# A hybrid decoder layer: two groups of turns issued sooner, three roots' Newton steps on GpSimd, the second gate weight and half of its projections in the first stage

## The chip, the cores and the metric

The kernel runs on one core of one Trainium2 chip. Its time is the device time of one execution in microseconds (us). Before the change the median of 3 runs is 1174.29 us (1173.09 to 1176.38). The engines are PE (TensorE), DVE (VectorE), ACT (ScalarE), POOL (GpSimd) and SP (SyncE, which here only issues DMAs). PEld is PE's loading of weights.

## The reference, cut to what matters

One sequence of 2048 rows with 1024 columns. A modulation is computed from `c`, the rows are normalised, and one wide projection feeds two attentions: eight heads of a forgetting attention (FoX) and eight query heads with two key and value heads of a sliding-window attention with a window of 128. Each branch is gated, and both go through one output projection.

```python
mod = jax.nn.silu(c) @ w_ada[l] + b_ada[l]
shift, scale, gate = jnp.split(mod, 3, axis=-1)
h = rms_norm(x, g_pre[l]) * (1.0 + scale[:, None, :]) + shift[:, None, :]
proj = h @ w_in[l]
qa, ka, va, fa, za, qb, kb, vb, zb = jnp.split(proj, split_points, axis=-1)
oa = forgetting_attention(qa, ka, va, fa + b_fgate[l]) * jax.nn.silu(za)
qb, kb = rope(qb, positions), rope(kb, positions)
ob = sliding_window_sink_attention(qb, kb, vb, sinks[l]) * jax.nn.silu(zb)
y = jnp.concatenate([oa, ob], axis=-1) @ w_out[l]
x = x + gate[:, None, :] * rms_norm(y, g_post[l])
```

What the change touches lies in the first stage: the root of `rms_norm`, the transposing of `h`, and the projections `kb` (keys), `vb` (values) and `zb` (gates of the sliding-window heads).

## The kernel before

**Precision.** Every fp32 operand of a large product is split into two f16 parts, a high and a low one, and a product is three matmuls (high by high, high by low, low by high) into one PSUM bank. A weight gets a power of two from its largest value as its scale, the rows `h` one from a bound on their size.

**Groups and units.** The 2048 rows are four groups of 512 (`ci` 0 to 3). A projection of one key (a weight of 128 columns: `kb`, `vb`, `zb0` to `zb3`, `qb0` and so on) for one group is eight units; a unit of `proj_units` (L325) is one k of 128 columns and three matmuls of 512 columns (L339). Behind the eighth unit stands an evacuation: `evac_rope` (L718) for keys and queries, with a copy on ACT, the cosine product on DVE, and seven ticks later the sine product (L746) with rows that a DMA has swapped; `evac_z` (L370) for gates, with a tanh on ACT (L383) and the product on DVE (L379), whose result POOL's queue stores to DRAM. A unit that holds a PSUM bank keeps it until its evacuation has read it; there are three such banks (`bk`).

**Turns.** `turn(ci, k)` (L418) brings one k of a group into the layout that the projections need: PE transposes four 128x128 tiles of the normalised rows `xt` into a PSUM tile `px` (L422, five of them), ACT scales and shifts them with `Gp` and `Shp` into `hf`, for even k also into the high part (L428), and DVE makes the low part by a subtraction (L433), for odd k after a cast to the high part (L432). Group 0's turns stand in the opening code: five are issued ahead of the code that computes `bmx`, `bm`, `pH`, `Gp` and `Shp` (its two small PE instructions are the transpose of `bmx` into bank 0 and the matmul of L644), and turns 5, 6 and 7 each follow when a `px` comes free. The turns of group ci+1 are strewn as extra units among the projections of group ci, at the places that the list `at_` gives.

**Root and normalisation.** ACT sums the squares of a group's rows (`squares`), `rsqrt_parts` (L97) takes the inverse root by an integer estimate and three Newton steps, on four columns, 13 operations of DVE in all. `root(ci)` runs it at one stroke; the root of group 1 is taken a step at a time between group 0's turns. `normal(ci)` multiplies the rows by the root, on DVE for groups 1 to 3.

**A weight's way.** Eight functions prepare a weight: `w_load` (L216, a DMA of POOL's queue), `w_max` (DVE takes the maximum of each partition, L222, and POOL's queue stores it to DRAM as `mx_d`, L225), `w_back` (POOL's queue loads it as a row on all partitions, `mxr`, L230), `w_scale` (DVE reduces the row, L241, and works out the scale), `w_high` (ACT, L256), two times `w_low` (DVE, L262) and `w_done`.

**What sets the order.** The order on each engine is the order of issue in the code. `add(key, units)` appends units to one long list `punits`. When a key is first added, its eight preparing functions are put into `events` at slots ahead of the first unit: 42, 31, 21, 12, 9, 7, 5 and 4 units ahead, for `qb0` and `zb1` the first four 16, 14, 12 and 4 sooner. `fill(n)` (L1083) runs the next n units, and ahead of each the functions that stand at its slot. In the first stage every second unit is followed by a `tick`, which runs what `after(n, f)` has put off by n ticks: the evacuations and the ACT and DVE halves of the turns. Squares, roots and normalisations of groups 2 and 3, and `spread` (the cosine and sine rows of a group), are events too.

**Stages.** The first stage has the list `kb`, `vb`, `zb0` for groups 0 to 2, `kb`, `vb` for group 3, then `qb0` for group 0, the rest of `zb0`, `qb0` for group 1, and the first group of `zb1`: 144 units, the 24 turns counted (`N_PRO`). In the profile it ends at 157 us. Then 32 windows of the sliding-window attention follow to 431 us. A window (`Pair`) has scores on PE (L871), maxima on DVE, exponentials on ACT (L893), transposes on PE (L900), their copy on ACT and a subtraction on DVE, four `affine_select` of POOL (L909, L911) and the product with the values on PE (L924); between these steps lie 296 units of the remaining `qb`, `zb`, and `va` projections, spread evenly over the 32 windows. The list `others` holds the `zb` and `va` projections in order, four per key: `zb0`, `zb1`, `va0`, `zb2`, `zb3`, `va1`, `va2`. The FoX stage and the output projection come behind.

Of the kernel before, what the change touches and what calls it, by code (L numbers as in the profile page):

```python
# [10 lines left out]
F32 = mybir.dt.float32  # L11
# [8 lines left out]
P = 128  # L20
# [23 lines left out]
def hybrid_layer(  # L44
# [46 lines left out]

    def rsqrt_mean(dst, ss, n):

        for _ in rsqrt_parts(dst, ss, n):
            pass

    def rsqrt_parts(dst, ss, n, more=None):  # L97
        v = sm(n, "rs_v")
        if more is None:
            V.tensor_scalar(v[:], ss, 1.0 / D, EPS, op0=ALU.mult, op1=ALU.add)  # L100
        else:
            V.scalar_tensor_tensor(v[:], ss, 1.0 / D, more, op0=ALU.mult, op1=ALU.add)
        y = sm(n, "rs_y")
        h = small.tile([P, n], I32, tag="rs_h", name="rs_h")
        V.tensor_scalar(h[:], v[:].bitcast(I32), 1, None, op0=ALU.logical_shift_right)
        V.tensor_scalar(y[:].bitcast(I32), h[:], -1, 0x5F3759DF, op0=ALU.mult, op1=ALU.add)
        V.tensor_scalar(v[:], v[:], -0.5, None, op0=ALU.mult)
        for it in range(3):
            yield
            t = sm(n, "rs_t")  # L110
            if n == 1:
                V.scalar_tensor_tensor(t[:], y[:], y[:], v[:], op0=ALU.mult, op1=ALU.mult)
            else:
                V.tensor_tensor(t[:], y[:], y[:], op=ALU.mult)
                V.tensor_tensor(t[:], t[:], v[:], op=ALU.mult)
            y2 = dst if it == 2 else sm(n, "rs_y")
            V.scalar_tensor_tensor(y2[:], t[:], 1.5, y[:], op0=ALU.add, op1=ALU.mult)
            y = y2
# [287 lines left out]
    def root(ci):  # L406
        ss, rst = rstd[ci]
        rsqrt_mean(rst, ss[:], 4)

# [7 lines left out]

    def turn(ci, k):  # L418

        px = ps_x.tile([P, CH], F32, tag="x", name="px")  # L420
        for u in range(4):
            PE.transpose(px[:, u * P:(u + 1) * P], xt[ci * 4 + u][:, k * P:(k + 1) * P], ident[:])  # L422
        hf = hst.tile([P, CH], F32, tag="hf", name="hf")
        hi, lo = hT[ci][:, 0, k, :], hT[ci][:, 1, k, :]

        def scaled():
            for dst in ([hi] if k % 2 == 0 else []) + [hf[:]]:
                A.activation(dst, px[:], AF.Identity, scale=Gp[:, k:k + 1], bias=Shp[:, k:k + 1])  # L428

        def split():  # L430
            if k % 2:
                V.tensor_copy(hi, hf[:])  # L432
            V.tensor_tensor(lo, hf[:], hi, op=ALU.subtract)  # L433

        return scaled, split
# [17 lines left out]
    with tc.manual_schedule():  # L453
# [186 lines left out]

        PE.transpose(bk[0][0:1, 0:P], bmx[:], ident[:])
        bm = st.tile([1, 1], F32, name="bm")
        V.tensor_reduce(bm[:], bk[0][0:1, 0:P], axis=AX.X, op=ALU.max)
# [6 lines left out]

        V.tensor_scalar(pfl[:], ipH[:], 0.5, None, op0=ALU.mult)
        root1 = rsqrt_parts(rstd[1][1], rstd[1][0][:], 4)
        for k in range(KT):
            turned[k][0]()
            turned[k][1]()
            if k >= 2:
                next(root1, None)
            if k + 5 < KT:
                turned.append(turn(0, k + 5))
        V.tensor_reduce(mxs[:, 2:3], wq["zb0"][0][:], axis=AX.XY, op=ALU.max, apply_absolute_value=True)  # L660
# [279 lines left out]
    def add(key, us):  # L940
        if key not in pkeys and key not in ("kb", "vb"):
            at = len(punits) - {"za3": 4}.get(key, 20 if key[:2] == "za" else 0)
            for n, (lead, f) in enumerate(((42, lambda: w_load(key, pieces(key))), (31, lambda: w_max(key)),
# [42 lines left out]
    for ci in range(NCH):  # L986
# [24 lines left out]
    add("qb0", qb_units(0, 1))  # L1011
    add(*others[4])
    N_PRO = len(punits)
    for n in range(4):
        at_slice(N_PRO + 20 + 3 * n, lambda: next(fx["sums"], None))
    qbs = [(f"qb{c_ // 4}", qb_units(c_ // 4, c_ % 4)) for c_ in range(2, 16)]
    n_o = 5
    for n, (key, us) in enumerate(qbs):
        add(key, us)
        lim = 5 + 5 * (n + 1) // 4 if n + 1 < len(qbs) else len(others)  # L1020
        for key2, us2 in others[n_o:lim]:
            add(key2, us2)
        n_o = lim
# [705 lines left out]
```

## Time and profile before

| | us |
|---|---|
| median of 3 runs | 1174.29 (1173.09 to 1176.38) |
| the profiled execution | 1176.95 |
| its span, first to last instruction | 1175.2 |
| PE busy | 1127.3 (96%) |
| DVE busy | 935.1 (80%) |
| ACT busy | 662.0 (56%) |
| POOL busy | 192.6 (16%) |

The page belongs to one profiled execution, 1176.95 us, which lies 2.66 us above the median; every time of the trace is of that execution. Times in a row of the timeline are the start in us from the span's start, then the duration in us, the engine, the line (L) of the kernel, the operation, and output<-input with partitions, elements and type; a bracket at the end gives the idle time ahead of the instruction and what ended it. A row of the groups has busy time and mean ns of one behind the first bar, and the idle time of the engine ahead of such instructions behind the second. The granted PE clock is what the chip's throttle let TensorE have, as a share of full speed.

### The profile page before, as it was taken

The page shows a single profiled execution, that of the slowest core. Times are in us where ns is not written, and L with a number is a line of the kernel's source. Part 1 is how long each engine was busy: PE and PEld are TensorE (multiplying, and loading weights), DVE is VectorE, ACT ScalarE, POOL GpSimd, SP SyncE. Part 2 cuts the span into 40 slices and gives each one's busy share as a digit, 9 for nine tenths or more (in the row PEclk, how much of TensorE's full clock was granted, in tenths as well). Part 3 has the DMA queues.
Part 4 walks back from the last instruction along what each step waited for, and adds up shares of the span by engine and source line. Part 5 has one row for each costly group of instructions (what it writes and reads, how often), then busy time and mean ns, then how long its engine had stood idle before and what let it go on. Part 6 is the DMA issues. An engine that isn't in the chain of part 4 may idle for free.

```text
span 1175.2 us, 26821 instructions
## 1 busy us (share of the span) xinstructions
PE 1127.3 (96%) x10637; PEld 671.1 (57%) x10637; DVE 935.1 (80%) x2167; ACT 662.0 (56%) x1150; POOL 192.6 (16%) x293
## 2 busy tenths in 40 slices
PE   5899999999899999999999999999999999999997
PEld 2465555755457986555555555555556555544444
DVE  7876668688786757788888999888897897778885
ACT  2784445454554531476766767666776788543332
POOL 1000135535445531001000100001000000000000
PEclk9899999999999999999999999999999999999999
DMA  9745433414324323513425422223311237586743
GB/s 332 280 124 87 78 93 73 91 51 106 90 65 89 73 43 75 81 47 95 74 66 60 111 43 74 61 44 73 52 33 47 68 86 231 137 213 199 195 144 108
DMA packets 123481, 120.19 MB, mean 102 GB/s; under 512 B 64948, under 2 KB 100828, under 8 KB 123356
## 3 DMA queue, kind: packets, MB, share of 16 engines
q1 hardware_dynamic: 112088, 85.69, 27.0%
q0 software_dynamic: 10832, 32.50, 13.8%
q8 instruction: 83, 1.36, 0.6%
q14 instruction: 42, 0.34, 0.1%
q10 hardware_dynamic: 436, 0.28, 0.1%
HBM read 64.75 MB, written 25.18 MB: 77 GB/s over the span
## 4 chain that ended last, share of the span: by engine, by line
PE 71%; DVE 11%; issue 8%; DMA 5%; ACT 2%; POOL 2%; SPq 0%; DVEq 0%; ACTq 0%; POOLq 0%
PE bk L339 24%; PE bk L1522 13%; PE bk L357 7%; PE sta L1311 4%; PE sta L1310 4%; PE bk L1261 4%; PE poa L1336 3%; PE poa L1337 3%; PE poa L1334 3%; DMA wa<-in_w_ada_dram 2%; PE pob L924 2%; PE pss L871 1%; DVE a_m L1264 1%; DVE pha L1324 1%; PE pxb L900 1%
## 5 line engine op out<-in xcount | busy, mean ns | idle before, releaser
L1317 ACT ACTIVATE p<-sta,lift,scl_qk 128x1024 f32<-128x1024 f32 (+2 forms) x160 | 171.8, 1074 | 131.8 <-PE sta L1311 82.7
L339 PE MATMUL bk<-hT,wh_qk 128*128 128x512 f16 x768 | 194.7, 378 | 0.0
L1324 DVE TENSOR_TENSOR pha<-p,pha 128x1024 f16<-128x1024 f32 (+2 forms) x160 | 169.0, 1056 | 0.2 <-ACT pha L1321 0.2
L1264 DVE TENSOR_REDUCE a_m<-bk 128x1 f32<-128x512 f32 x192 | 130.3, 685 | 46.8 <-PE bk L1261 45.8
L1522 PE MATMUL bk<-wohl,oz 128*128 128x512 f16 x744 | 165.3, 379 | 1.0 <-DVE oz L1471 0.7
L1321 ACT ACTIVATE pha<-p 128x1024 f16<-128x1024 f32 (+2 forms) x160 | 148.1, 926 | 5.9 <-PE poa L1337 1.2
L1522 PEld LDWEIGHTS <-oz 128*128 128x128 f16 x744 | 71.8, 99 | 82.8 <-DVE oz L1471 1.8
L1337 PE MATMUL poa<-vt,pha 128*128 128x65 f16 x1088 | 116.1, 192 | 1.4 <-DVE pha L1324 1.4
L1334 PE MATMUL poa<-vt,pha 128*128 128x65 f16 x1088 | 116.6, 193 | 0.8 <-DVE ona L1343 0.7
L1336 PE MATMUL poa<-vt,pha 128*128 128x64 f16 x1088 | 116.6, 194 | 0.0
L339 PEld LDWEIGHTS <-wh_qk 128*128 128x128 f16 x768 | 72.2, 97 | 74.4 <-issue 1.9
L1310 PE MATMUL sta<-T 128*128 128x512 f16 (+1 forms) x320 | 110.9, 346 | 2.8 <-ACT p L1317 2.7
L1261 PE MATMUL bk<-T 66*128 66x512 f16 (+2 forms) x320 | 109.7, 348 | 3.2 <-DVE a_m L1264 1.9
L1334 PEld LDWEIGHTS <-pha 128*128 128x128 f16 x1088 | 101.5, 96 | 15.5 <-DVE ona L1343 1.9
L1311 PE MATMUL sta<-T 69*128 69x512 f16 (+1 forms) x320 | 109.8, 348 | 0.0
L1336 PEld LDWEIGHTS <-pha 128*128 128x128 f16 x1088 | 100.9, 97 | 11.4
L1337 PEld LDWEIGHTS <-pha 128*128 128x128 f16 x1088 | 100.8, 99 | 1.8 <-DVE pha L1324 1.8
L339 PE MATMUL bk<-hT,wh_za 128*128 128x512 f16 x384 | 99.7, 378 | 0.0
L357 PE MATMUL bk<-wh_va,hT 128*128 128x128 f16 x1536 | 89.9, 219 | 0.0
L357 PEld LDWEIGHTS <-hT 128*128 128x128 f16 x1536 | 87.1, 98 | 4.1 <-issue 2.1
L339 PE MATMUL bk<-hT,wh_zb 128*128 128x512 f16 x384 | 89.0, 380 | 0.0
L339 PE MATMUL bk<-hT,wh_qb 128*128 128x512 f16 x384 | 87.4, 379 | 0.0
(447 smaller groups left out, 1917.7 us busy)
## 6 DMA issues: line engine op xcount, KB each, us to landing
hT<-in_x_dram SPq DMA_DIRECT2D x20, 512.0 KB
wa<-in_w_ada_dram SPq DMA_DIRECT2D x16, 512.0 KB
z_d<-tz POOLq DMA_DIRECT2D x32, 256.0 KB, 3.0
T<-stq SPq DMA_DIRECT2D x64, 128.0 KB
T<-z_d SPq DMA_DIRECT2D x16, 512.0 KB
out_dram<-hT SPq DMA_DIRECT2D x15, 512.0 KB
xt<-in_x_dram SPq DMA_DIRECT2D x12, 512.0 KB
qs<-qf SPq DMA_DIRECT2D x80, 64.0 KB
```

What stands on the lines that cost most here:

```text
L339: PE.matmul(ps, whl[:, a, k, :], hT[ci][:, b, k, :], start=(k == 0 and n == 0), stop=(k == KT - 1 and n == 2))
L357: PE.matmul(ps[:, u * P:(u + 1) * P], hT[ci][:, a, k, u * P:(u + 1) * P], whl[:, b, k, :], start=(k == 0 and n == 0), stop=(k == KT - 1 an ...
L1261: PE.matmul(mx[:, :w], T[0:XM, 0, i * P:(i + 1) * P], T[0:XM, 2, pc * CH:pc * CH + w], start=True, stop=True)
L1310: PE.matmul(self.st[:, o:o + w], T[:, 3, kb_], T[:, 1, qc], start=True, stop=False)
L1311: PE.matmul(self.st[:, o:o + w], T[0:XR, 2, kb_], T[0:XR, 0, qc], start=False, stop=not diag)
L1317: A.activation(self.p32[:, :self.w], self.st[:, :self.w], AF.Exp, scale=scl[f"qk{self.hd}"][:], bias=lift[:])
L1321: A.activation(self.ph[:, 0, :self.w], self.p32[:, :self.w], AF.Copy)
L1324: V.tensor_tensor(self.ph[:, 1, :self.w], self.p32[:, :self.w], self.ph[:, 0, :self.w], op=ALU.subtract)
L1334: PE.matmul(po[:, u, :], ph[:, 0, pq], vt[:, b, hd, 0:65], start=(self.first and n == 0 and u == 0), stop=False)
L1336: PE.matmul(po[:, u, 0:64], ph[:, 0, pq], vt[:, b, hd, 65:VW], start=False, stop=False)
L1337: PE.matmul(po[:, u, :], ph[:, 1, pq], vt[:, b, hd, 0:65], start=False, stop=(self.last and n == len(self.blocks) - 1))
L1522: PE.matmul(py, self.hl[:, i, k, :], w_slot(8 * j + k)[:, cc], start=(k == 0 and m_ == 0), stop=(k == KT - 1 and m_ == 2))
```

## The change

Four edits, all in the order and the place of work; the matmuls stay the same.

1. Two of group 0's turns, k = 5 and 6, are issued right behind the transpose of `bmx`, into the PSUM banks 1 and 2 in place of a `px`; the turn of k = 7 follows behind the first turn's DVE half.
2. The roots of groups 1, 2 and 3 take their first three operations on DVE and the rest on GpSimd. The operation that adds 1.5 and multiplies becomes two there, so a root has 13 operations on GpSimd. Group 1's root is issued at one stroke ahead of group 0's turns, no longer step by step between them. Group 2's root moves from 13 to 18 slots ahead of the end of group 0's list, its normalisations stay; group 3's root stays, and its normalisations move from the end of group 1's list to 6 slots ahead of it.
3. The weight `zb1` is prepared at fixed slots: load at 14, maximum at 38, the row back at 44, scale at 50, high part at 53, low parts at 55 and 57, the rest at 59.
4. The projections of `zb1` for groups 0 and 1 stand behind `zb0` of groups 1 and 2. Its group 2 stays behind `qb0` where group 0 of it was; `zb0` of group 3 stays where it was, and group 3 of `zb1` goes into the windows' list with the others. So the first stage has 160 units and the windows share 280. The turns of group 3 take the places of those of group 2.

```diff
-    def rsqrt_parts(dst, ss, n, more=None):
+    def rsqrt_parts(dst, ss, n, more=None, eng=None):
+        W = eng or V
...
-        V.tensor_scalar(v[:], v[:], -0.5, None, op0=ALU.mult)
+        W.tensor_scalar(v[:], v[:], -0.5, None, op0=ALU.mult)
...
-                V.tensor_tensor(t[:], y[:], y[:], op=ALU.mult)
-                V.tensor_tensor(t[:], t[:], v[:], op=ALU.mult)
+                W.tensor_tensor(t[:], y[:], y[:], op=ALU.mult)
+                W.tensor_tensor(t[:], t[:], v[:], op=ALU.mult)
...
-            V.scalar_tensor_tensor(y2[:], t[:], 1.5, y[:], op0=ALU.add, op1=ALU.mult)
+            if eng is None:
+                V.scalar_tensor_tensor(y2[:], t[:], 1.5, y[:], op0=ALU.add, op1=ALU.mult)
+            else:
+                W.tensor_scalar(t[:], t[:], 1.5, None, op0=ALU.add)
+                W.tensor_tensor(y2[:], t[:], y[:], op=ALU.mult)
...
     def root(ci):
         ss, rst = rstd[ci]
-        rsqrt_mean(rst, ss[:], 4)
+        rsqrt_mean(rst, ss[:], 4, G if ci else None)
...
-    def turn(ci, k):
-
-        px = ps_x.tile([P, CH], F32, tag="x", name="px")
+    def turn(ci, k, px=None):
+
+        px = px or ps_x.tile([P, CH], F32, tag="x", name="px")
...
         PE.transpose(bk[0][0:1, 0:P], bmx[:], ident[:])
+        turned += [turn(0, k, bk[k - 4]) for k in (5, 6)]
         bm = st.tile([1, 1], F32, name="bm")
...
-        root1 = rsqrt_parts(rstd[1][1], rstd[1][0][:], 4)
+        root(1)
         for k in range(KT):
             turned[k][0]()
             turned[k][1]()
-            if k >= 2:
-                next(root1, None)
-            if k + 5 < KT:
-                turned.append(turn(0, k + 5))
+            if k == 0:
+                turned.append(turn(0, 7))
...
-                if n < 4 and key in ("qb0", "zb1"):
+                if n < 4 and key == "qb0":
                     lead += (16, 14, 12, 4)[n]
+                if key == "zb1":
+                    lead = at - (14, 38, 44, 50, 53, 55, 57, 59)[n]
...
             add(*others[ci])
+            if ci:
+                add(*others[3 + ci])
...
-            at_ = ([14, 16, 17, 18, 19, 20, 21, 22], [6, 8, 10, 12, 14, 16, 18, 20], [6, 7, 9, 10, 12, 13, 15, 16])[ci]
+            at_ = ([14, 16, 17, 18, 19, 20, 21, 22], [6, 8, 10, 12, 14, 16, 18, 20], [6, 8, 10, 12, 14, 16, 18, 20])[ci]
...
-                    at_slice(len(punits) - (0 if ci else 10) + u, lambda ci=ci, u=u: normal(ci + 2, (u,)))
-                at_slice(len(punits) - 13, lambda ci=ci: root(ci + 2))
+                    at_slice(len(punits) - (6 if ci else 10) + u, lambda ci=ci, u=u: normal(ci + 2, (u,)))
+                at_slice(len(punits) - (13 if ci else 18), lambda ci=ci: root(ci + 2))
...
-    add(*others[4])
+    add(*others[6])
...
-    n_o = 5
+    n_o = 7
...
-        lim = 5 + 5 * (n + 1) // 4 if n + 1 < len(qbs) else len(others)
+        lim = 7 + 5 * (n + 1) // 4 if n + 1 < len(qbs) else len(others)
```

More of the change, by code (lines that the diff above doesn't have):

```diff
@@ L90, in pow2_floor, with rsqrt_mean @@
         V.tensor_scalar(dst.bitcast(I32), t[:].bitcast(I32), 0x7F800000, None, op0=ALU.bitwise_and)
-    def rsqrt_mean(dst, ss, n):
-        for _ in rsqrt_parts(dst, ss, n):
-            pass
-    def rsqrt_parts(dst, ss, n, more=None):
+    def rsqrt_mean(dst, ss, n, eng=None):
+        for _ in rsqrt_parts(dst, ss, n, eng=eng):
+            pass
+    def rsqrt_parts(dst, ss, n, more=None, eng=None):
+        W = eng or V
         v = sm(n, "rs_v")
@@ L111, in rsqrt_parts @@
             if n == 1:
-                V.scalar_tensor_tensor(t[:], y[:], y[:], v[:], op0=ALU.mult, op1=ALU.mult)
+                W.scalar_tensor_tensor(t[:], y[:], y[:], v[:], op0=ALU.mult, op1=ALU.mult)
             else:
-                V.tensor_tensor(t[:], y[:], y[:], op=ALU.mult)
-                V.tensor_tensor(t[:], t[:], v[:], op=ALU.mult)
+                W.tensor_tensor(t[:], y[:], y[:], op=ALU.mult)
+                W.tensor_tensor(t[:], t[:], v[:], op=ALU.mult)
             y2 = dst if it == 2 else sm(n, "rs_y")
-            V.scalar_tensor_tensor(y2[:], t[:], 1.5, y[:], op0=ALU.add, op1=ALU.mult)
+            if eng is None:
[3 more added lines that the diff above has]
+                W.tensor_tensor(y2[:], t[:], y[:], op=ALU.mult)
             y = y2
```

## The prediction

> **What bounds the kernel now.** I read first the page's span and the chain that ended last, then the busy times cut at the borders of the stages that the change touches. A row of that second view is the stretch, its length, then the busy time of PE, PEld, DVE, ACT and POOL, and after them the granted PE clock, the DMA share and GB/s.
>
> ```profile
> span 1175.2 us, 26821 instructions
> PE 71%; DVE 11%; issue 8%; DMA 5%; ACT 2%; POOL 2%; SPq 0%; DVEq 0%; ACTq 0%; POOLq 0%
> 42.00:56.00 14.00, 10.85 (x48) 6.11 (x49) 10.92 (x35) 8.76 (x15) 0.00 (x0) 0.76 0.49 157
> 70.00:78.00 8.00, 6.61 (x33) 3.31 (x34) 7.90 (x14) 6.81 (x10) 0.00 (x0) 1.00 0.28 67
> 97.00:101.00 4.00, 1.76 (x8) 0.77 (x7) 4.00 (x7) 0.18 (x1) 0.56 (x1) 1.00 0.42 121
> 115.00:131.00 16.00, 13.57 (x124) 9.20 (x123) 11.15 (x29) 5.31 (x10) 1.09 (x2) 0.89 0.46 97
> 157.00:431.00 274.00, 266.88 (x3167) 183.51 (x3166) 203.39 (x458) 137.34 (x430) 136.37 (x200) 0.99 0.33 76
> ```
>
> PE carries the chain, and the change removes no matmul and adds none. So time can only come from PE's idle stretches and from its half clock. The rows show where these lie: DVE is the full engine at 70 to 78 (7.90 of 8) and at 97 to 101 (4.00 of 4), while PE idles 1.39 and 2.24 us. At 115 to 131 PE idles 2.43 us and its clock is granted at 0.89, which is another 0.11 x 16 = 1.8 us. The sliding-window stage, 157 to 431, idles 7.1 us. The sum below is made against the profiled execution: 1176.95 us, of which 1.75 lie outside the span.
>
> **Two turns sooner, root of group 1 (42 to 56).**
>
> ```profile
> 39.47 2.35 PE L422 MATMUL px<-ident,xt 128*128 128x128 f32 x20
> 43.03 0.38 PE L644 MATMUL bk<-bm,ones 1*128 1x1 f32 x2 [0.37 <-DVE bm L643]
> 44.49 0.78 ACT L428 ACTIVATE hT<-px,Shp,Gp 128x512 f16<-128x512 f32 x1 [2.17 <-DVE pfl L651]
> 51.12 1.50 ACT L428 ACTIVATE hf<-px,Shp,Gp 128x512 f32<-128x512 f32 x2
> 54.92 1.21 DVE L660 TENSOR_REDUCE mxs<-wr_zb 128x1 f32<-128x1024 f32 x1
> ```
>
> Eight transposes go ahead of the matmul of L644, on which Gp and all of ACT's work hang. At 2.35 / 20 = 0.12 us each they take 0.9 us, of which 0.4 fill the gap in front of L644, so ACT starts 0.5 us later. ACT then works without a break, 44.49 to 52.62, and becomes the bound: it ends near 53.1, and DVE's last cast and subtraction (0.42 and 0.69, rows below) at 54.2. Before, DVE ended at 54.92, because ten small operations of the root lay between its subtractions. Gain 0.8 us; it is not more, since ACT hides the rest. Bounds: 0, if the transposes run at half clock, and 1.3, if they delay nothing.
>
> **Root of group 2 (64 to 78).**
>
> ```profile
> 64.37 0.16 DVE L100 TENSOR_SCALAR rs_v<-ss 128x4 f32<-128x4 f32 x1
> 66.54 0.16 DVE L117 SCALAR_TENSOR_TENSOR rst<-rs_t,rs_y 128x4 f32<-128x4 f32 x1
> 66.82 0.69 DVE L746 TENSOR_TENSOR qs<-qs,sinT 128x512 f32<-128x512 f32 x1
> L433 DVE TENSOR_TENSOR hT<-hf,hT 128x512 f16<-128x512 f32 x32 | 21.8, 690 | 9.6 <-ACT hf L428 8.9
> L432 DVE CAST hT<-hf 128x512 f16<-128x512 f32 x16 | 6.7, 420 | 0.0
> 7.16 0.29 POOL L534 TENSOR_SCALAR_AFFINE_SELECT triu<-ones 128x128 f32<-128x128 f32 x1
> 159.43 0.63 POOL L909 TENSOR_SCALAR_AFFINE_SELECT ptb<-fold 128x512 f16<-128x512 f16 x1 [2.20 <-ACT fold L914]
> ```
>
> The two root rows are the first and last of 13 operations, 2.3 us. Three stay on DVE (0.6); ten leave, 1.7 us. PE idles 1.39 us there, so at most that comes back: I take 1.2, with 0 if the sine (L746) then waits for its DMA instead. GpSimd gets 13 operations in one dependent chain, as the addition of 1.5 becomes an operation of its own. No row shows such a small one on four columns. Below: DVE's own 0.16 us. Above: 0.63 us for 512 columns. From 0.29 for 128 columns to 0.63 for 512 the line goes to 0.18 at four; I take 0.22, near the lower end, so 2.9 us a chain. Up to there it is hidden: DVE has the sine, the bias product and a split to do before the first normalisation. All three chains find POOL empty, except as below.
>
> The Trainium skill, GPSIMD Engine Reference, section 8, says that elementwise work is about twice as fast on DVE and that both share SBUF interfaces; at twice DVE's 0.2 us start to start a chain would be 5.2 us and cost the sum about 1 us. No row here shows these operations on GpSimd.
>
> **Second gate weight sooner, its projections behind groups 2 and 3.** Eight units of PE work (5.2 us) move from 157-431 to about 90, eight more to about 122. That alone is neutral; what it fills and what it waits for is not.
>
> ```profile
> 78.32 0.69 DVE L379 SCALAR_TENSOR_TENSOR tz<-tz,bk 128x512 f32<-128x512 f32 x1 [0.24 <-ACT tz L383]
> 121.03 1.21 DVE L222 TENSOR_REDUCE w_mx<-wr_zb 128x1 f32<-128x1024 f32 x1
> 101.81 0.54 POOL L225 DMA_DIRECT2D mx_d<-w_mx  x1 [1.91 <-DVE w_mx L222]
> 102.38 0.90 POOL L216 DMA_DIRECT2D wr_zb<-in_w_in_dram  x1
> 110.63 0.55 POOL L230 DMA_DIRECT2D mxr<-mx_d  x1 [7.35 <-DMA mx_d<-w_mx]
> 165.99 0.56 POOL L230 DMA_DIRECT2D mxr<-mx_d  x1 [2.18 <-DMA mx_d<-w_mx]
> 170.62 0.29 DVE L241 TENSOR_REDUCE w_mx<-mxr 128x1 f32<-128x128 f32 x1 [0.25 <-DMA mxr<-mx_d]
> DMA to landing us min/median/max: 7.6/8.2/8.4
> 123.22 0.28 DVE L241 TENSOR_REDUCE w_mx<-mxr 128x1 f32<-128x128 f32 x1
> 124.10 0.15 DVE L248 TENSOR_SCALAR w_sw<-w_sw 128x1 f32<-128x1 f32 x1
> 62.12 1.41 DVE L262 SCALAR_TENSOR_TENSOR wh_zb<-wr_zb,w_sw,wh_zb 128x512 f16<-128x512 f32 x2 [0.41 <-ACT wh_zb L256]
> 92.56 4.70 PE L339 MATMUL bk<-hT,wh_kb 128*128 128x512 f16 x21
> ```
>
> A weight's maximum goes to DRAM and comes back as a row. From the issue of the one DMA to the issue of the other pass 8.8 us (101.81 to 110.63), and 4.6 more to the reduction (165.99 to 170.62). The landing row is that of the stores of the maximum from 90 to 320 us. The change leaves six slots, about 4 us, for each way. In DVE's new order the maximum of zb1 stands right behind the tz of 78.32, which comes about 2.3 us sooner: 76.0, the maximum ends at 77.9, its store is issued at 78.2, the load at 87.0, the row is there at 91.6. DVE comes to the reduction near 86 and stands. Queued behind it are five splits of group 2, the sine of kb, and the low halves of zb1; on ACT the high half of zb1 with the value evacuation and the rest of group 2; on POOL the load of the row stands ahead of root 3 and the load of qb0. The scale takes 1.0 us (123.22 to 124.25), then come a cast, two subtractions and the two sine operations (2.9 us) and the first low half (0.7): 96.2. PE arrives 2.0 us before today's 92.56, at 90.5, and can do two matmuls (0.4). It waits 96.2 - 90.5 - 0.4 = 5.3 us, and a wait of that size costs clock: I take 1.8 us, the loss at 115 to 131. Together **+7.1 us**. Bounds: 0, if the maximum is 5 us sooner, and 9, with the longest landing and a second stretch of half clock.
>
> The Trainium skill, DMA: Bandwidth & Descriptors, section "Anatomy of one DMA", gives a fixed cost of about 2 us for such a DMA. By it this wait would be almost nothing; the rows above, 8.2 us in the median, disagree.
>
> **What comes back behind it.**
>
> ```profile
> 100.62 0.81 PE L339 MATMUL bk<-hT,wh_kb 128*128 128x512 f16 x3
> 116.89 0.69 DVE L746 TENSOR_TENSOR qs<-qs,sinT 128x512 f32<-128x512 f32 x1 [7.94 <-DMA cosT<-cs__234]
> ```
>
> From 97.26 to 100.62 PE does four transposes (0.4 us) and otherwise waits for DVE's normalisation of group 3. With 12 us more on PE ahead of that point (5.2 of work, 7.1 of waiting), it is ready, even at a late chain on POOL: **-2.9 us**. The stall at 115 to 131 begins with DVE standing 7.94 us for a transfer of the sine, issued while the zb1 load of 102.38 follows right behind the store of a maximum. In the new order no weight load follows such a store within 8 us in this stage, and eleven units instead of seven lie between the last turn and the kb that needs it: 2.43 + 1.8 = **-4.2 us**; bounds 0 and -4.2.
>
> **The sliding-window stage.**
>
> ```profile
> 130.78 5.34 PE L339 MATMUL bk<-hT,wh_qb 128*128 128x512 f16 x24
> 135.96 5.34 PE L339 MATMUL bk<-hT,wh_zb 128*128 128x512 f16 x24
> 300.03 0.75 DVE L262 SCALAR_TENSOR_TENSOR wh_zb<-wr_zb,w_sw,wh_zb 128x512 f16<-128x512 f32 x1 [2.07 <-ACT wh_zb L256]
> 302.28 0.28 DVE L241 TENSOR_REDUCE w_mx<-mxr 128x1 f32<-128x128 f32 x1
> 309.24 0.26 PE L924 MATMUL pob<-vb,ptb 128*128 128x64 f16 x3 [2.19 <-POOL ptb L909]
> 310.27 1.09 PE L924 MATMUL pob<-vb,ptb 128*128 128x64 f16 x19 [0.78 <-POOL ptb L911]
> ```
>
> A unit is 5.18 / 8 = 0.65 us. The 32 windows share 280 units instead of 296: half a unit, 0.33 us, less cover in each. Against that, where two weights were prepared at once (zb and qb at 300: both splits on DVE, then PE 3.0 us idle, then matmuls at half clock, about 1.7 us), they now lie 40 units apart; the pair at 240 to 258 parts as well. A new pair, va0 and qb1, arises at the start of the stage. I take 3.0 + 1.7 + 1.5 back for the two pairs, 1.5 lost on the new one and 1.2 on thinner windows: **-3.5 us**, between -8.8 (all idle and the lost clock) and +10.4 (every window is short by 0.33).
>
> **Sum:** -0.8 - 1.2 + 7.1 - 2.9 - 4.2 - 3.5 = -5.5, so 1171.5 from the profiled execution. That one stands 2.7 us over the median of the runs, 1174.29; some of its idle time may be its own. From the median it would be 1168.8. I forecast between them: **1170 us**.
>
> **Rivals.** (1) The weight is there in time: without the 7.1, 1163. For it: six slots were left on each way. Against it: the landing row. (2) GpSimd is late: at 0.63 us a chain is 8.2 us, the normalisations come 3 to 5 us later, the 1.2 and the 2.9 are gone: 1174. Against it: the 128-column row. (3) The windows eat what they gain (0 in place of -3.5, or a little worse): 1174.5. For it: POOL's ptb ends most waits there. (4) Slower: the windows are bound by their own chain (scores, maxima, fold, selects), not by PE. Then the filler moved out shortens nothing, and each bound window gives back 0.33 us: with all 31, 1170 + 3.5 + 10.4 = 1184. It decides from about 13 windows on: 1170 + 3.5 + 4.3 = 1177.8. Against it: 7.1 us of idle time in 274. (5) The change as worded does nothing, since ACT is the bound where DVE is relieved: that is the 0.8, counted above.
>
> **How the numbers follow.** Forecast 0.47 (own range 1166 to 1174), rival 1 0.12, rival 2 0.10, rival 3 0.18, rival 4 0.13. About 0.3% (3.5 us) is what a measurement can tell from no change: faster means under 1170.8, slower over 1177.8. Faster: 0.33 of the forecast's 0.47 and rival 1, 0.45. Slower: rival 4 and the end of rival 3, 0.18. Same: 0.37. The range reaches from rival 1 into rival 4: 1163 to 1178.
>
> **What would show it.** The reduction of mxr for zb1 stands on DVE for about 5 us, ended by the DMA, and PE's first zb1 matmuls wait near 90 to 96; the idle stretches of 70 to 78, 97 to 101 and 115 to 131 are gone; root chains on POOL last about 3 us; in the windows the idle time before L924 falls below 7.1 us, and no half clock near 310. Wrong it would be if that idle time grows, or if DVE does not stand.

## The result: 0.5% slower, and what the profile after shows

The changed kernel takes 1180.24 us in the median of 5 runs (1177.59 to 1182.41), the kernel before 1174.29 in 5 (1173.09 to 1176.38). The ratio is 1.0047, with a 95% interval of 1.0035 to 1.0058: slower, where a faster kernel was forecast, and outside the range of the prediction (1163 to 1178). A second comparison gave 1.0040 (1.0022 to 1.0059).

One thing is to be kept in mind while reading the traces. The profiled execution of before took 1176.95 us, above all five of its runs; that of the changed kernel took 1177.59, the shortest of its five. The two traces differ by 0.6 us, the medians by 6.0. The traces show which waits came and went; what each costs in a usual execution is a matter of the experiments.

The page of the changed kernel, span and chain:

```profile
span 1175.9 us, 26838 instructions
...
PE 73%; DVE 12%; DMA 5%; issue 4%; POOL 2%; ACT 2%; SPq 1%; ACTq 0%; DVEq 0%; POOLq 0%
```

Busy times of the changed kernel in the stretches of the prediction and in 92 to 98 us; columns as there (length, then PE, PEld, DVE, ACT, POOL, granted PE clock, DMA share, GB/s):

```profile
42.00:56.00 14.00, 10.53 (x55) 5.43 (x53) 10.69 (x29) 8.66 (x14) 4.44 (x13) 0.88 0.60 195
70.00:78.00 8.00, 6.52 (x33) 3.10 (x32) 7.68 (x13) 5.45 (x8) 0.38 (x1) 1.00 0.51 132
92.00:98.00 6.00, 1.81 (x6) 0.39 (x5) 5.33 (x15) 3.56 (x7) 0.00 (x0) 0.94 0.15 41
97.00:101.00 4.00, 3.79 (x10) 1.39 (x11) 3.86 (x14) 2.81 (x5) 0.28 (x2) 0.57 0.15 35
115.00:131.00 16.00, 16.00 (x102) 9.01 (x100) 9.48 (x24) 6.69 (x12) 1.80 (x4) 1.00 0.36 83
157.00:431.00 274.00, 264.27 (x3126) 181.11 (x3125) 203.14 (x463) 137.96 (x436) 135.36 (x197) 0.99 0.33 73
```

The idle time at 97 to 101 has gone except for 0.2 us, but PE runs at a clock of 0.57 there. The stall at 115 to 131 has gone, half clock and all. PE still idles 1.48 us at 70 to 78 (before 1.39), a new hole of 4.2 us stands at 92 to 98, and the sliding-window stage idles 9.7 us instead of 7.1. PE's idle time ahead of the product with the values (L924 before, L928 now), which the prediction named as the place to look, has fallen, from 7.0 to 5.4 us, and no half clock follows near 310. What has come is elsewhere: 2.3 us of waiting for DVE ahead of projections of va0, and 1.9 us for which the profile names nothing.

How the two traces stand at the same piece of work is read from two landmarks: the first projection of `qb0`, which ends the first stage's projections of groups 0 to 3 (130.78 in the trace of before, shown above), and the first matmul behind the windows. First the changed kernel's two, then the second of before:

```profile
139.24 5.34 PE L344 MATMUL bk<-hT,wh_qb 128*128 128x512 f16 x24
436.09 0.25 PE L1226 MATMUL bk<-identh,lk 128*72 128x128 f16 x1 [0.40 <-DVE lk L1246]
```

```profile
434.33 0.25 PE L1218 MATMUL bk<-identh,lk 128*72 128x128 f16 x1 [0.41 <-DVE lk L1238]
```

The changed kernel has 16 units more behind it at the first landmark, 16 x 0.648 = 10.4 us. It is there 8.5 us later, so 1.9 us ahead. From there to the second landmark it takes 296.85 us for 10.4 us less of work, before took 303.55: it loses 3.7 us. **In these two traces the first stage gains what was forecast; the sliding-window stage loses what the first stage gained, and more.** Behind the second landmark the changed kernel gets 1.1 us back, which is not accounted for. A second pair of traces, taken for the experiments below, has the landmarks at 131.91 and 438.54 us before and at 141.99 and 440.74 changed. There the first stage gains only 0.3 us and the rest loses 2.5, so the loss in the windows is in both pairs and the size of the gain ahead of them is not.

Two new stands in the sliding-window stage can be seen. The first is DVE's, for the row of va0:

```profile
165.16 0.54 POOL L230 DMA_DIRECT2D mx_d<-w_mx  x1 [0.58 <-DVE w_mx L227]
165.69 0.54 POOL L235 DMA_DIRECT2D mxr<-mx_d  x1
...
177.18 0.29 DVE L246 TENSOR_REDUCE w_mx<-mxr 128x1 f32<-128x128 f32 x1 [6.51 <-DMA mxr<-mx_d]
...
181.66 0.94 PE L362 MATMUL bk<-wh_va,hT 128*128 128x128 f16 x14 [1.68 <-DVE tz L384]
183.22 0.72 PE L362 MATMUL bk<-wh_va,hT 128*128 128x128 f16 x10 [0.62 <-DVE wh_va L267]
```

The chain of waits puts it in one row, the start, the length and the transfer:

```profile
165.69 11.46 DMA mxr<-mx_d
```

A row lands 4.3 to 5.2 us after its issue where the trace shows it elsewhere. This one takes 11.5: 0.5 us ahead of it in POOL's queue goes the store of the maximum of qb1. A larger store (256 KB of `z_d`) stands 1.7 us ahead of it, but a row 0.8 us behind such a store alone, at 330 us, lands after 5.2. DVE stands 6.5 us, PE idles 4.0 us between 180 and 186. Not all of that is new: the trace of before has 1.3 us of idle time at 182 to 184.

The second is PE's own at 404 us, where the profile names no releaser ("issue"). Two issues of POOL, then the stretch behind them, then PE's row:

```profile
393.60 0.55 POOL L230 DMA_DIRECT2D mx_d<-w_mx  x1
394.14 1.79 POOL L221 DMA_DIRECT2D wr_qk<-in_w_in_dram  x2
```

```profile
396.00:403.00 7.00, 7.00 (x137) 7.00 (x136) 4.66 (x11) 3.53 (x13) 4.38 (x6) 1.00 0.92 27
```

```profile
405.58 0.72 PE L875 MATMUL pss<-kst,stb 64*128 64x256 f16 x9 [1.92 <-issue]
```

Again a transfer, here the load of the weight qk0, stands 0.5 us behind the store of a maximum. For seven microseconds the DMA engines are 92% busy and move 27 GB/s. One DMA queue carries instructions in packets of 16 KB; by its rhythm it is PE's. In it no packet starts between 390.7 and 403.1 us. 469 records of PE (matmuls and weight loads) lie in that time, where 190 to 310 lie between its other packets of 370 to 440 us, but for 41 right behind the late one. PE then idles as if it had run out of instructions.

### The profile page after: what moved, and what is told of

Its sections match the earlier page's. It is cut to its first block, busy times and chain, and to the rows that moved or that the text cites. A ratio compares the mean times of both kernels' runs of the same rounds, so it can differ in the third digit from the quotient of the medians.

```text
span 1175.9 us, 26838 instructions
## 1 busy us (share of the span) xinstructions
PE 1128.7 (96%) x10637; PEld 670.4 (57%) x10637; DVE 929.3 (79%) x2137; ACT 662.4 (56%) x1150; POOL 207.1 (18%) x332
## 4 chain that ended last, share of the span: by engine, by line
PE 73%; DVE 12%; DMA 5%; issue 4%; POOL 2%; ACT 2%; SPq 1%; ACTq 0%; DVEq 0%; POOLq 0%
PE bk L344 27%; PE bk L1530 12%; PE bk L362 5%; PE sta L1319 4%; PE sta L1318 4%; PE bk L1269 4%; PE poa L1344 3%; PE poa L1345 3%; PE poa L1342 3%; DMA wa<-in_w_ada_dram 2%; PE pss L875 2%; PE pob L928 1%; DVE a_m L1272 1%; DVE pha L1332 1%; DMA mxr<-mx_d 1%
```

## The experiments

Theory 1, after the traces: the change costs two waits for a row, zb1's at 92 and va0's at 177, and each brings a stretch of half clock with it. Theory 2 is rival 4 of the prediction: the windows have too little cover everywhere. Theory 3: the loss is a matter of the clock in executions that the first profile does not show. All ratios are against the kernel before, run on the same chip in between; what a kernel gains on the changed one is the difference of two such ratios, times 1178 us, and is uncertain by 2 to 3 us. The absolute times in the first expectations are at the level of the first comparison, 3.6 us lower than here.

**Both kernels again.** No edit.

> The kernel before, profiled a second time. The first profiled execution took 1176.95 us, 2.7 over the median of 1174.29, with five half-clock stretches that cost PE 11.9 us of clock. Theory 1 (the change costs two waits for a weight's row, which every execution has) expects the same idle stretches in the second trace, about 1174 us, and the same number of half-clock stretches give or take one. Theory 3 (the loss of the change lies in half-clock stretches that its profiled execution happened not to have) expects fewer stretches here than in the changed kernel: a mean granted clock of 0.993 against 0.990.

> The changed kernel again. Its profiled execution took 1177.59 us, the shortest of its five, while the longest took 1182.41. Theory 1 (two waits for a row, of 4.2 and 4.0 us of PE idle, each with a half-clock stretch of 1.7 us behind it) expects both waits again within 0.5 us of their sizes, and 1178 to 1182 us. Theory 3 expects that executions of 1181 and more carry one to three half-clock stretches more than the first profile's five, at a mean granted clock of 0.988 to 0.990, and that the time follows the clock at 1.7 us a stretch.

Before: 1179.07 us, ratio 1.0005 (0.9989 to 1.0020). Changed: 1182.73 us, 1.0040 (1.0022 to 1.0059). The waits are there again, 5.6 us at 92 to 99, which is 1.4 more than the first time and not within the 0.5 expected, and 4.3 at 182 to 190. What differs besides is the clock behind them. First the first trace of the changed kernel, then the second:

```profile
97.00:105.00 8.00, 7.79 (x29) 3.18 (x30) 5.93 (x17) 3.50 (x6) 3.38 (x13) 0.79 0.29 68
185.00:194.00 9.00, 8.23 (x113) 6.80 (x113) 7.99 (x21) 5.27 (x15) 2.85 (x4) 0.81 0.21 55
```

```profile
97.00:105.00 8.00, 6.29 (x16) 2.33 (x17) 7.43 (x19) 3.88 (x6) 2.31 (x7) 0.57 0.22 52
185.00:194.00 9.00, 7.02 (x79) 5.61 (x79) 8.00 (x21) 4.33 (x12) 4.15 (x6) 0.62 0.11 38
```

A clock of 0.79 over 8 us is 1.7 us lost, 0.57 is 3.4: the half clock comes in pieces of 3.41 us, one piece behind each wait in the first trace, two in the second. So the first trace had the mildest form of both. Theory 3 is right in part: the executions differ by the clock, but in the changed kernel it is the clock behind the two waits. The trace of before of this pair is near the top of its own runs, 1181.23 us at a mean clock of 0.987, so the pair of traces again shows little of the difference.

**Row of va0 ahead of qb1's store.** Load, maximum and row of va0 go eight slots sooner.

```diff
+                if n < 3 and key == "va0":
+                    lead += 8
```

> Changed kernel with load, maximum and row of va0 eight slots sooner, so that its row no longer stands in POOL's queue right behind the store of qb1's maximum. Theory 1 expects DVE's stand of 6.5 us at 177 and PE's 4.0 us of idle at 180 to 186 to go, the half clock behind it too: 4 to 5.7 us less than the changed kernel, 1174 to 1176. Theory 2 (the windows are short of cover everywhere, since 280 units instead of 296 lie between their steps) expects idle time to move to other windows and at most 1 us: 1179 to 1180.

1179.26 us, 1.0010 (0.9996 to 1.0025): 3.5 us less than the changed kernel, a little under what theory 1 expects and clearly over the 1 us of theory 2. The row stands 6.7 us ahead of the store, and DVE no longer stands for it:

```profile
159.24 0.55 POOL L235 DMA_DIRECT2D mxr<-mx_d  x1 [5.10 <-DMA mx_d<-w_mx]
165.94 0.54 POOL L230 DMA_DIRECT2D mx_d<-w_mx  x1 [0.58 <-DVE w_mx L227]
...
171.35 0.26 DVE L246 TENSOR_REDUCE w_mx<-mxr 128x1 f32<-128x128 f32 x1
```

Of PE's 4.0 us of idle time at 180 to 186, 0.8 are left; 1.5 us stand at 191 to 193, about what the kernel before has at 182 to 184. So little moved to other windows, not all of it as theory 2 wanted. In this trace the stand at 404 us is 3.84 us long and a half clock of two pieces follows, which takes back part of the gain.

**The same store in SP's queue.**

```diff
-        G.dma_start(md[:], mx[:])
+        (SP if key == "qb1" else G).dma_start(md[:], mx[:])
```

> Changed kernel with one transfer in another queue: the store of qb1's maximum is issued by SP instead of POOL, so that the row of va0 no longer stands behind it in POOL's queue; all else is at its place. If the row waits because a queue works in order, it lands 4.3 to 5 us after its issue, DVE stands 0 to 1 us in place of 6.5, and the kernel is 4 to 5.7 us faster than the changed one. If the store holds the DMA engines themselves, whatever the queue, the row still lands 10 us or more after its issue, DVE's stand stays over 5 us, and the time stays within 1 us.

1178.44 us, 1.0002 (0.9989 to 1.0016): 4.5 us less than the changed kernel by the ratios.

```profile
165.47 0.54 POOL L235 DMA_DIRECT2D mxr<-mx_d  x1
```

```profile
165.81 0.33 SPq L230 DMA_DIRECT2D mx_d<-w_mx  x1
```

```profile
173.80 0.29 DVE L246 TENSOR_REDUCE w_mx<-mxr 128x1 f32<-128x128 f32 x1 [1.87 <-DMA mxr<-mx_d]
```

Neither reading is borne out in full. The row lands 8.3 us after its issue: sooner than 11.5, later than 5, although the store, in the other queue, was issued 0.3 us behind it. DVE stands 1.9 us, and that is short enough for PE. Standing behind the store in its queue is about half of the delay in these two traces; that the other half comes from what both queues share is argued. The Trainium skill, DMA: Bandwidth & Descriptors, section "Issuing engines are not separate DMA queues", says that transfers of all issuing engines end on the same 16 engines, so that another issuer saves only issue time. The trace agrees in so far as the row is still 3 to 4 us late with the store in another queue. But the other queue saved 3.2 us of the row's way, and an issue takes 0.5.

**Nothing waits for zb1's row.** Its two projections go behind group 2, row and scale later.

```diff
-            if ci:
-                add(*others[3 + ci])
+            if ci == 2:
+                add(*others[4])
+                add(*others[5])
...
-                    lead = at - (14, 38, 44, 50, 53, 55, 57, 59)[n]
+                    lead = at - (14, 38, 58, 84, 87, 89, 91, 93)[n]
```

> Changed kernel with both of zb1's projections in the first stage behind group 2, row and scale of zb1 later by 14 and 34 slots, so that nothing waits for the row; the windows' units stay as changed. Theory 1 expects PE's 4.2 us of idle at 92 to 97 and the half clock behind them to go; the 2.2 us at 97 to 101 of the kernel before may come back, since eight units less lie ahead of the first turns of group 3: 3.5 to 5.9 us less than the changed kernel, 1174.5 to 1177. Theory 2 expects the loss to lie in the windows, which are the same here: DVE then only moves its stand, and the time falls by under 2 us, 1178 to 1180.

1179.26 us, 1.0007 (0.9989 to 1.0025): 3.9 us less by the ratios. PE is busy 6.34 of the 7 us where it had idled; 1.35 us of the idle time at 97 of the kernel before come back. The stand for va0's row is here too, and longer, so the two waits are separate:

```profile
90.00:97.00 7.00, 6.34 (x31) 2.83 (x29) 6.63 (x13) 3.89 (x6) 2.88 (x7) 1.00 0.49 110
...
173.65 0.29 DVE L246 TENSOR_REDUCE w_mx<-mxr 128x1 f32<-128x128 f32 x1 [7.77 <-DMA mxr<-mx_d]
```

**Load of qk0 ahead of a store.**

```diff
-            for n, (lead, f) in enumerate(((42, lambda: w_load(key, pieces(key))),
+            for n, (lead, f) in enumerate(((42 + 6 * (key == "qk0"), lambda: w_load(key, pieces(key))),
```

> Changed kernel with the load of the weight qk0 six slots sooner, so that it stands ahead of the store of a maximum at 393 us in POOL's queue and not 0.5 us behind it. In the traces of the changed kernel PE idles 1.9 and 2.6 us at 404 to 410 with no releaser shown, while the load's packets take up to 7.3 us and the fetch of PE's instructions starts only at 403.1. Theory: the store stops the engines, the load behind it piles up, the fetch comes late. It expects the idle 2 to 3 us, and half clock behind it in some runs, to go: 2 to 4 us less than the changed kernel. If PE's instructions run out there because of how many the windows hold, whatever the transfers, the idle time stays and the time is within 1 us.

1179.19 us, 1.0010 (1.0001 to 1.0019): 3.5 us less by the ratios.

```profile
408.48 0.43 PE L875 MATMUL pss<-kst,stb 64*128 64x256 f16 x2 [1.00 <-issue]
```

The stand with no releaser is down to 1.0 us, not gone; that explains 0.9 to 1.6 us against the two traces of the changed kernel, and not the whole 3.5. With the load behind the store it was 1.92, 2.62, 3.84, 3.51 and 1.65 us in five traces, with half clock behind two of them; in the sixth, with qb1's store in SP's queue, the place showed none and another stand of 2.2 us came at 417. That the store keeps back the load, and the load the fetch of instructions, is argued from the transfers and from this; the fetch was not tested alone.

**The same in the kernel before.** There the load of zb1 stands 0.6 us behind the store of qb0's maximum.

```diff
-            for n, (lead, f) in enumerate(((42, lambda: w_load(key, pieces(key))),
+            for n, (lead, f) in enumerate(((42 + 12 * (key == "zb1"), lambda: w_load(key, pieces(key))),
```

> Kernel before, with nothing but the load of zb1 12 slots sooner, so that it stands ahead of the store of qb0's maximum and no longer 0.6 us behind it. In the traces of before DVE stands 7.9 us for a cosine row and PE idles 2.0 to 2.4 us at 119 to 124, with a half clock behind. If the store holds the engines and the load behind it keeps the cosine rows back, the stall goes: 2.4 us of idle and 1.7 us of clock, 3 to 4 us less than before, at 0.9965 to 0.9975 of it. If the stall has another cause (the cosine rows are issued too late anyway, or their buffer is not free), it stays, and the time is within 1 us of before.

1176.34 us, 0.9981 (0.9970 to 0.9992): 2.2 us less, under the 3 to 4 expected. DVE's stand of 7.94 us, which its row puts down to a transfer of the cosine and not of the sine, is down to 1.5, and the stall at 115 to 131 is gone with nothing else changed:

```profile
110.80 0.69 DVE L746 TENSOR_TENSOR qs<-qs,sinT 128x512 f32<-128x512 f32 x1 [1.52 <-DMA sinT<-sn__233]
```

```profile
115.00:131.00 16.00, 16.00 (x146) 10.36 (x144) 9.01 (x36) 3.21 (x7) 1.63 (x3) 1.00 0.38 71
```

So the largest single gain of the change, the 4.2 us at 115 to 131 in the first trace, does not need the change: moving one load takes that stall away. Two rows of this trace still stand right behind a store, at 223 and 283 us; they land after 7.8 and 8.5 us. So such a place costs a row about 3 us there, and not the 7 of va0.

**Roots on DVE.**

```diff
-        rsqrt_mean(rst, ss[:], 4, G if ci else None)
+        rsqrt_mean(rst, ss[:], 4)
```

> Changed kernel with all four roots on DVE again, at the changed kernel's places. In the changed kernel's trace the chain of root 2 took 6.0 us on POOL, with operations of 0.2 us beside an idle DVE and 0.6 us beside a busy one, and DVE stood 0.96 us for it; the load of zb1 stands behind it in POOL's queue. Theory 1 expects the roots to be nearly neutral: the normalisation of group 2 starts 0.3 us later to 0.7 us sooner, the load of zb1 goes 6 us sooner without use, and the time stays within 1 us of the changed kernel, 1181.7 to 1183.7 at the level of this chip's last runs. The theory that GpSimd is what costs (rival 2 of the prediction) expects 2 to 4 us less.

1186.40 us in 6 runs, 1.0074 (1.0054 to 1.0094): slower than the changed kernel, against both expectations. The trace does not show why: it is of the shortest of the six executions, and its span is 1179.9 us, 0.9 less than the second trace of the changed kernel. What it does show is a half clock of three pieces (a clock of 0.53 over 11 us, 5.2 us lost) behind the wait for va0's row, where the changed kernel had one and two:

```profile
183.00:194.00 11.00, 8.70 (x89) 7.33 (x89) 9.91 (x24) 5.28 (x15) 5.20 (x7) 0.53 0.17 53
```

The same edit was therefore made again further down, in a kernel without the waits.

**The first two edits alone.** The kernel before with the turns and the roots as changed and the rest as before.

> Kernel before with two parts of the change alone: the two turns sooner, the roots of groups 1 to 3 on GpSimd with group 2's five slots sooner; zb1, its projections, the normalisation of group 3 and the places of its turns stay as before. The prediction has -0.8 and -1.2 us for these: 2.0 us under before, a ratio of 0.9983. The trace of the changed kernel gives -0.6 to -0.8 for the turns and -0.3 for root 2, since the chain on POOL took 6.0 us and DVE stood for it: about 1 us, 0.999. If root 3, which then also runs late on POOL ahead of the normalisation at 97 us, costs more there than it takes off DVE, the 2.2 us of idle time at 97 to 101 grow to 4 or more, and the ratio is 1.000 or above.

1174.21 us, 0.9964 (0.9949 to 0.9978): a gain of 4.2 us, twice the prediction's 2.0 and four times what the traces gave. The idle time at 97 to 101 fell to 1.3 us without any unit moved; the rest is not accounted for by its trace.

**Three mends together**, of zb1's place, va0's and qk0's transfers, as above.

> Changed kernel with three mends together: both zb1 projections of the first stage behind group 2, with row and scale later; load, maximum and row of va0 eight slots sooner; load of qk0 six slots sooner. Apart they stood 3.5, 3.5 and 3.5 us under the changed kernel (ratios 1.0007, 1.001 and 1.001 against its 1.004). If the three losses are separate waits, they add up: 8 to 11 us under the changed kernel, a ratio of 0.995 (0.993 to 0.997) against the kernel before, and no idle stretch over 1.5 us in the first 430 us. If one wait only hides another, the ratio stays at 0.998 or above and a new stretch of over 2 us shows up.

1168.39 us (1167.74 to 1168.46), 0.9917 (0.9901 to 0.9932): 10 us under the kernel before, better than the expected 0.993 to 0.997, and, by the ratios, 14.5 under the changed one. The sum of the three apart is 3.9 + 3.5 + 3.5 = 10.9; the intervals are too wide to tell the two apart.

```profile
span 1166.0 us, 26836 instructions
```

```profile
157.00:431.00 274.00, 267.59 (x3179) 183.65 (x3178) 205.88 (x475) 138.84 (x437) 137.96 (x200) 1.00 0.32 75
...
396.00:406.00 10.00, 10.00 (x187) 9.57 (x184) 7.95 (x22) 6.26 (x18) 5.22 (x9) 1.00 0.22 35
```

The windows now idle 6.4 us, less than before (7.1), with the same 280 units: theory 2 is refuted. The clock is 1.00 over the whole stage. No half clock is left between 51 us and the last 5 us of the kernel, and the runs lie within 0.7 us, where the kernel before spreads over 7 on this chip. If the excess over the sum is real, the half clocks behind the waits that each single mend left standing would explain it; that is not shown.

**The same with the roots on DVE.**

> The kernel with the three mends, and all roots on DVE. Theory 1: the trace of the changed kernel with roots on DVE had the first projection of group 1 complete its inputs 0.7 us later, and no other stretch longer, so GpSimd is worth 0.5 to 1 us and this kernel lies at most 1 us over the one with the three mends. The rival takes the medians at their word: the changed kernel with roots on DVE stood at 1.0074 against 1.004, so the roots on GpSimd are worth 3 to 4 us, and this kernel lies 3 to 4 us over the one with the mends.

1170.17 us (1169.15 to 1170.86), 0.9931 (0.9917 to 0.9945). The runs of the two kernels do not overlap: the roots on GpSimd are worth 1.8 us, between the two expectations. The trace has it in one row, here first with the roots on DVE, then on GpSimd:

```profile
97.00:105.00 8.00, 6.75 (x53) 5.22 (x53) 5.82 (x10) 2.82 (x4) 1.45 (x2) 0.79 0.46 119
```

```profile
97.00:105.00 8.00, 7.31 (x97) 6.39 (x96) 5.80 (x12) 5.27 (x9) 1.45 (x2) 1.00 0.47 117
```

With root 3 on DVE the idle stretch in front of group 3 is 1.8 us instead of 1.3, and a half clock follows it.

**The kernel before, mended alike.** The load of zb1 goes 12 slots sooner, load, maximum and row of zb3 and of qb2 8 slots, nothing else.

> Kernel before with nothing but events moved: load of zb1 12 slots sooner, load, maximum and row of zb3 and of qb2 8 slots sooner, so that no load and no row stands within 1 us behind the store of another maximum before 390 us. The first alone gave 0.9981. If what counts is only which transfer stands behind a store, the idle time of 3.0 us at 307 and the half clock behind it go as well: 0.994 to 0.995, and the change itself is worth nothing beyond its mends. If the change's own parts are worth something, this kernel stays at 0.996 to 0.998, above the changed kernel with its three mends.

1177.57 us, 0.9997 (0.9981 to 1.0014), though its profiled execution took 1172.46, the shortest of its 12 (the longest 1182.28). That trace has no half clock between 52 us and its last 6, and the stall at 307 has shrunk from 3.0 to 1.4 us. What its longer executions have is not seen. The gain of 2.2 us from the first of these moves, above, does not show here, though the move is in it; the two intervals overlap. So what such moves are worth in the kernel before stays open. They are not enough to reach the changed kernel with its three, which lies 9 us lower; so it is not the moved transfers alone that make that one fast.

## Why the prediction was wrong

**The step that failed** is the last term, the sliding-window stage: -3.5 us, in which the new pair va0 and qb1 stood at 1.5. By the landmarks the stage was +3.7 in the first pair of traces and +2.5 in the second. By idle time and clock of the first pair, part by part:

- The new pair, taken at 1.5: 4.0 us of idle time where 1.3 stood before, and 1.7 of clock, so about 4.4. In the second trace it was 4.3 and 3.4.
- The load of qk0 behind a store, taken at nothing: 1.9 us at 404. The shift of the windows' list brought it too, and it was not foreseen at all.
- The pair at 240 to 258, taken at -1.5: 0.1, as 1.6 us of idle time stand at 258 to 268 instead.
- The pair at 300, taken at -4.7: right, -4.4. PE idles 0.7 us at 291 to 300, and no half clock follows.
- Thinner windows, taken at 1.2: about 0.7, as 1.1 us stand in three places at 346 to 387 where 0.4 stood.

That is +2.7 of the +3.7; the rest is not placed.

The prediction quoted the right row, the maximum's way of 8.8 us, and counted that way for zb1; for the new pair it took a price by feel and did not lay out POOL's queue. `w_back` of va0 falls at slot 163 and `w_max` of qb1 at 161, which the slots alone tell.

**The other terms**, against the traces:

- The turns, -0.8: right. From the transpose of `bmx` to the first `vb` matmul the changed kernel takes 0.8 us less, and ACT is the bound, as said.
- Root 2, -1.2: wrong in size. From the first `vb` matmul to the last matmuls of `kb` for group 1 the changed kernel takes 0.2 and 0.5 us less in the two pairs of traces, about -0.3. The chain on POOL took 6.0 us, not 2.9:

```profile
63.13 0.23 POOL L108 TENSOR_SCALAR rs_v<-rs_v 128x4 f32<-128x4 f32 x1 [11.89 <-DVE rs_h L106]
63.33 0.63 POOL L115 TENSOR_TENSOR rs_t<-rs_y 128x4 f32<-128x4 f32 x1
64.03 0.20 POOL L116 TENSOR_TENSOR rs_t<-rs_t,rs_v 128x4 f32<-128x4 f32 x1
...
68.89 0.20 POOL L122 TENSOR_TENSOR rst<-rs_t,rs_y 128x4 f32<-128x4 f32 x1
```

```profile
69.12 1.74 DVE L421 TENSOR_SCALAR xt<-xt,rst 128x1024 f32<-128x1024 f32 x2 [0.96 <-POOL rst L122]
```

  An operation takes 0.20 to 0.23 us while DVE is idle and up to 0.65 beside it. The 0.22 of the prediction was the price beside an idle DVE, and DVE then stands 0.96 us for the result. The Trainium skill, GPSIMD Engine Reference, section 8, which the prediction weighed, says that the two share SBUF interfaces and that DVE is about twice as fast. The trace fits the sharing, and the 5.2 us a chain that the prediction estimated from the page was nearer than its own 2.9.
- Weight zb1, +7.1: right in mechanism, and within its bounds. (The landing row quoted for it was not of the stores from 90 to 320 us alone, as the prediction says, but of all 23 of the trace, from 101.8 to 835.3 us.) The store is issued at 80.14, the row at 88.14, DVE stands until 92.46:

```profile
80.14 0.54 POOL L230 DMA_DIRECT2D mx_d<-w_mx  x1 [0.56 <-DVE w_mx L227]
88.14 0.54 POOL L235 DMA_DIRECT2D mxr<-mx_d  x1 [7.47 <-DMA mx_d<-w_mx]
92.46 0.28 DVE L246 TENSOR_REDUCE w_mx<-mxr 128x1 f32<-128x128 f32 x1 [4.79 <-DMA mxr<-mx_d]
94.75 0.60 PE L344 MATMUL bk<-hT,wh_zb 128*128 128x512 f16 x2 [2.32 <-ACT wh_zb L261]
97.21 6.60 PE L344 MATMUL bk<-hT,wh_zb 128*128 128x512 f16 x22 [1.86 <-DVE wh_zb L267]
```

  4.2 us of idle time and 1.7 of clock, 5.9; 5.6 and 3.4, 9.0, in the second trace. Its removal alone gave 3.9 us, since 1.35 us of idle time came back.
- Group 3's normalisation, -2.9: 2.0 came. PE idled only 2.24 us at 97 to 101 by the prediction's own row, so the term was too large from the start.
- The stall at 115, -4.2: it came in full, 2.43 us of idle time and 1.8 of clock.

The first stage adds up to -2.0 in the prediction and to -1.9 in the first pair of traces, -0.3 in the second. The agreement in the first is partly luck: the wait for zb1 was 1.2 us shorter than forecast and the gains of root 2 and the normalisation together 1.8 smaller, and the terms as read here add up to -1.4.

**The second thing that failed** is the base. The sum was made against one execution and moved half-way to the median. Behind each new wait stands a half clock of one or two pieces in the two traces, 1.7 or 3.4 us; the prediction counted one behind zb1's and none behind va0's. How many pieces a usual execution has is not shown, so it stays open how the 0.6 us between the first two traces become 6.0 between the medians.

The rivals: rival 4 had the right sign, by a mechanism that is refuted (280 units cover the windows as well as 296 did, once the transfers are in order). Rival 3 had the right place. Rival 2 was right that the chain on GpSimd is late, 6.0 us between the 2.9 forecast and its 8.2, and yet GpSimd wins by 1.8 us.

## What to carry to other kernels

When work is moved along a list, lay out the slow queue's new order, not only the engines': look for every load and every read-back that now stands right behind a small store to DRAM, and put them ahead of it. Here that, with the place of zb1's projections, took the changed kernel from 1.004 of the kernel before to 0.992; in the kernel before the same was worth 2.2 us with one load and nothing that could be measured with three weights. A wait of 2 us or more on TensorE mostly cost its length and 1.7 us of clock or more behind it, and how much differed from trace to trace. A sum made against one trace needs the spread of the runs beside it before its sign is trusted.

## What was not expected of the hardware

- A store of 128 x 4 bytes to DRAM lands 6.9 to 8.1 us after its issue (7.6 in the median, changed kernel, 60 to 440 us). Behind one, a load of 512 KB moved at 27 GB/s with the engines 92% busy, and a row load of 64 KB landed after 11.5 us instead of 4.3 to 5.2 (7.8 and 8.5 at two places of the kernel before with one load moved).
- PE seems to run out of instructions in such a time: 1.7 to 3.8 us of idle time in five traces that the profile puts down to nothing. The cause is argued, not shown.
- Idle stretches of 1.8 us and more on PE were mostly followed by half clock, in pieces of 3.41 us; stretches of up to 1.5 us were not. It isn't strict: behind the 1.9 and 2.6 us at 404 to 410 in the two traces of the changed kernel there was none, behind 2.2 us at 97 to 101, in four parts, three of four traces with the order of before had none, and in the kernel before with one load moved 3.0 us at 305 to 308 had none. The Trainium skill, TensorE: Matmul & The Clock Gate, section "Part 1: The HAM clock gate", describes a free-running window of 3413 ns, and half clock after an idle one. The length of the pieces agrees, and a window that runs freely would explain why executions differ; no run here tests that. An idle window was not needed here: with the three mends and the roots on DVE, 1.8 us within 4 were enough.
